# Modulation loads from GpSimd's queue, and seven modulation steps behind each second-gate tile of a two-layer hybrid block

## The chip, the cores and the metric

The kernel runs on one core of one Trainium2 chip. The metric is the device time of one execution in microseconds (us), as the median of three runs. The engines are named as in the profile: PE (TensorE, matmuls), PEld (its weight loads), DVE (VectorE), ACT (ScalarE), POOL (GpSimd) and SP (SyncE, which here only issues DMAs). A q behind an engine's name, as in SPq, is the DMA issue of that engine.

## What is computed

Two layers act on 512 latent tokens and 256 context tokens of width 1024. Each layer derives six modulation vectors per stream from a condition vector, and then computes a gated mixer of three branches and a gated MLP. Cut to what matters here:

```
m = jax.nn.silu(cond) @ ada_w[l] + ada_b[l]          # 6 x 1024, for c and for c_ctx
hx = modulate(rms_norm(x, norm1_g[l]), shift1, scale1)
z  = split_in(hx @ w_in[l])                          # conv, attention, gMLP and 3 x 1024 gate inputs
gates = sigmoid(z_gates + gate_b)
m = gates[0] * y_conv + gates[1] * (attn @ attn_out) + gates[2] * y_sgu
x = x + gate1 * (m @ w_o)
x = x + gate2 * conv_ffn(modulate(rms_norm(x, norm2_g[l]), shift2, scale2))
```

The context stream goes through the first layer whole, and in the second only gives keys and values.

## The kernel before

**Matmuls.** Activations lie with channels on the partitions. Every product is made of three matmuls (lines 468 to 470: high by high, low by high, high by low), so each weight tile is split on chip into a high part, copied by ACT (line 114), and a low part, subtracted by DVE (line 117). Raw weights come in pieces of 1 MB on SP's queue (`load8`, `load4`, `load_ao`, lines 162 to 176) into two buffers named `raw`; the split parts go to a ring named `hl`.

**The stretch that the change touches.** In layer 0 the mixer goes: attention for six tiles of 128 tokens with other matmuls filled in between, then the second gate (`gate(1, j, sg[j])`, eight output tiles j, each with 24 matmuls over 512 latent columns and 24 over 256 context columns), then the product of the attention with `attn_out` (`gated`, eight tiles with half as many matmuls each), then `w_o`. A gate tile ends with an activation by ACT. An `attn_out` tile ends on DVE: line 120 takes it out of PSUM (rows named `g<-g,x` for the 512 latent columns, `g<-g,c` for the 256 context columns), adds it to `m` and splits it for `w_o`. There are two PSUM buffers x and one buffer c here, so the matmuls of the context columns of tile j+1 can start only when DVE has taken tile j out of c.

**The modulation steps.** Only the first vectors of layer 0 are made by matmuls at the start. The others are dot products on DVE, put in behind PE's work: a step loads 128 rows of the transposed weights by 512 columns (256 KB, `t<-in_adat`) into one of four buffers named `t`, and DVE multiplies it with a row of silu that was broadcast over the partitions (`srow<-sd`, also 256 KB, one buffer), and sums it up. Two generators do this. `ada_apart` (lines 342 to 362) makes blocks 16 to 35 of layer 0, first for the context and then for the latent condition, in two halves each: 4 x 20 = 80 steps, with a new `srow` every 20. `ada` (lines 328 to 340) makes blocks 36 to 47 of layer 0 and all blocks of layer 1, later in the program.

**What sets the order.** A call `tick(n)` advances the running generator by n steps; `paced` ties a step to the place of the last matmul written. A scheduler then lays the instructions of every engine out in one fixed order, and each engine and each DMA queue works through its own order without overtaking. In layer 0 the 80 steps of `ada_apart` are ticked 24 times behind the third gate (in the attention), 6 times behind each of the eight second-gate tiles, and once behind each of the eight `attn_out` tiles:

```
        for j in range(8):
            gate(1, j, sg[j])
            tick(6)
        ...
            ms.append((hi, lo))
            tick(1)
        drain()
```

The weight loads of the steps are issued by SP, between the loads of the raw weights; the rows of silu are issued by ACT. GpSimd does nothing but fill 20 small buffers with zeros (line 915, `qT`, for the scores of the attention).

Of the kernel before, what the change touches and what calls it, by code (L numbers as in the profile page):

```python
# [79 lines left out]
def body(tc, I, out):  # L80
    nc = tc.nc
# [8 lines left out]
    def T(p, shape, dt, tag, bufs):  # L90
        return p.tile(shape, dt, tag=tag, name=tag, bufs=bufs)
# [24 lines left out]
    def tt(o, a, b, op):  # L116
        V.tensor_tensor(out=o, in0=a, in1=b, op=op)  # L117
# [13 lines left out]
    def split(hi, lo, src):  # L131
        acopy(hi, src)
        tt(lo, src, f(hi), sub)
# [88 lines left out]
    def page(tag, bufs, dt=F32, n=NT):  # L222
        return T(sp, [128, n], dt, tag, bufs)
# [12 lines left out]
        nc.scalar.dma_start(out=ff, in_=I["ff"][l])  # L236
        return ff

    def bcast_in(t, src):
        nc.scalar.dma_start(out=t, in_=src.unsqueeze(0).broadcast_to([128, src.shape[0]]))  # L240

    def load_rows(l):
        tab = page("t", NTP)
        nc.scalar.dma_start(out=tab[:, :512], in_=I["cst"][:, 512:1024])
        tabC = tab[:, :256].rearrange("p (t d) -> p t d", t=4)
        tabS = tab[:, 256:512].rearrange("p (t d) -> p t d", t=4)
        g = page("t", NTP)
        gq = T(cp, [128, 64], F32, "gq", 1)
        bcast_in(g[:, 0:136], I["qk"][l])
        nsk = T(cp, [128, 8], F32, "nsk", 1)  # L250
        ts(nsk, g[:, 128:136], -1.0, mul)
        ts(gq, g[:, 0:64], 0.125, mul)
        tabs = []
        for i in range(2):
            gg = g[:, 64:128] if i else gq
            tb = T(cp, [128, 512], F32, "tabq", 1) if i == 0 else page("t", NTP)
            tC = tb[:, :256].rearrange("p (t d) -> p t d", t=4)
            tS = tb[:, 256:512].rearrange("p (t d) -> p t d", t=4)
            tt(tC, tabC, gg.unsqueeze(1).broadcast_to([128, 4, 64]), mul)
            for h in range(2):  # L260
                o = lambda t: t.rearrange("p t (a h d) -> p t a h d", a=2, h=2)[:, :, :, h, :]
                gv = gg.rearrange("p (a h d) -> p a h d", a=2, h=2)[:, :, 1 - h, :]
                for t in range(4):
                    tt(o(tS)[:, t], o(tabS)[:, t], gv, mul)
            tabs.append((tC, tS, gg))
        return dict(nsk=nsk, q=tabs[0], k=tabs[1])
# [10 lines left out]
    sd = T(dp, [2, D], F32, "sd", 1)  # L277
# [49 lines left out]
    def ada(l, pool, blocks, both):  # L327

        for h in range(2):
            sr = T(pool, [128, 2, 512], F32, "srow", 1)  # L330
            for c in range(2):
                bcast_in(sr[:, c], sd[c, h * 512:h * 512 + 512])
            for j in blocks:
                w = page("t", NTP)
                nc.sync.dma_start(out=w[:, :512], in_=I["adat"][l, j, :, h * 512:h * 512 + 512])
                yield
                for c in ((1, 0) if j in both else (0,)):
                    o = mods[l][c][:, j:j + 1]
                    paced(V.tensor_tensor_reduce(out=w[:, 512:].bitcast(BF16) if c else w[:, :512], in0=w[:, :512], in1=sr[:, c], scale=1.0,
                                                 scalar=o if h else adab[l][:, j:j + 1], op0=mul, op1=add, accum_out=o))  # L340
                yield

    def ada_apart(l, pool, blocks):


        steps = [(c, h, j) for c in (1, 0) for h in range(2) for j in blocks]

        def load(j, h):
            w = page("t", NTP)
            nc.sync.dma_start(out=w[:, :512], in_=I["adat"][l, j, :, h * 512:h * 512 + 512])  # L350
            return w

        w = load(blocks[0], 0)
        for i, (c, h, j) in enumerate(steps):
            if j == blocks[0]:
                sr = T(pool, [128, 512], F32, "srow", 1)
                bcast_in(sr, sd[c, h * 512:h * 512 + 512])
            yield
            o = mods[l][c][:, j:j + 1]
            paced(V.tensor_tensor_reduce(out=w[:, :512], in0=w[:, :512], in1=sr, scale=1.0,  # L360
                                         scalar=o if h else adab[l][:, j:j + 1], op0=mul, op1=add, accum_out=o))
            if i + 1 < len(steps):
                w = load(steps[i + 1][2], steps[i + 1][1])
# [13 lines left out]
    def tick(n=1):  # L377
        for _ in range(n):
            while bgs:
                try:  # L380
                    g = bgs[0]
                    next(g)
                    if g in bgs:
                        bgs.append(bgs.pop(bgs.index(g)))
                    break
                except StopIteration:
                    bgs.remove(g)

    def drain(g=None):
        while bgs if g is None else g in bgs:  # L390
            tick()
# [4 lines left out]
    def paced(r):  # L396

        if last[0] is not None:
            tc.add_manual_dep(r.ins, last[0].ins.name, SCHED)
# [160 lines left out]
    for l in range(2):  # L560
# [88 lines left out]
        def ab_load(i):  # L649
            if i == 0 and full:  # L650
                ab_load.raw = [raw_tile() for _ in range(2)]
                for h in range(2):
                    for b in range(2):
                        nc.sync.dma_start(
                            out=ab_load.raw[b].rearrange("p (k c) -> p k c", k=8)[:, :, h * 128:h * 128 + 128],
                            in_=I["w_in"][l, :, b * 512 + h * 128:b * 512 + h * 128 + 128].rearrange("(k p) c -> p k c", p=128))
            elif i % 2 == 0:
                ab_load.raw = [load8(I["w_in"][l], b * 512 + i * 128) for b in range(2)]
            PRI[0] = 300
            return [subA(r, i % 2) for r in ab_load.raw]  # L660

        w, t = ab_load(0), page("t", NTP)
# [98 lines left out]
        def gate(b, j, dst):  # L761
            for _ in gate_steps(b, j, dst):
                pass
# [14 lines left out]
        def gated(*a):  # L778
            for _ in gated_steps(*a):
                pass  # L780
# [74 lines left out]
        def Pc_steps():  # L855
            for j in range(8):
                yield from gated_steps(m[j], I["conv_out"][l], j, cv)

        def Gs_steps():
            for j in range(8):  # L860
                t = page("t", NTP) if j >= 2 else early[j]
                if j >= 2:
                    yield from gate_steps(2, j, t)
                tick(2)
                yield from gated_steps(t, I["sgu_out"][l], j, ys)
                tt(m[j][:, :n_m], m[j][:, :n_m], t[:, :n_m], add)
                tick(1)
# [4 lines left out]
        src = [Pc_steps(), Gs_steps()]  # L872
# [138 lines left out]
        if l == 0:  # L1011
            start(ada_apart(0, ap_, range(16, 36)))
# [34 lines left out]
        sg = [sg[j // 2][:, (j % 2) * 768:(j % 2) * 768 + 768] for j in range(8)]  # L1047
        for j in range(8):
            gate(1, j, sg[j])
            tick(6)  # L1050
        Os = list(zip(Oh, Ol))
        ms = []
        for j in range(8):
            gated(sg[j], I["attn_out"][l], j, Os, True)
            tt(m[j][:, :n_m], m[j][:, :n_m], sg[j][:, :n_m], add)
            hi, lo = page("y", 8, F32R), page("m", 8, F32R) if j else page("t", NTP, F32R)
            split(hi[:, :n_m], lo[:, :n_m], m[j][:, :n_m])
            ms.append((hi, lo))
            tick(1)
        drain()  # L1060
        pa.close()

# [32 lines left out]
        if l == 0:  # L1095
            ag = start(ada(0, fp_, range(36, 40), range(48)))
# [22 lines left out]
        if l == 0:  # L1119
            ag = start(ada(0, fp_, range(40, 48), range(48)))  # L1120
# [90 lines left out]
        for ch in range(1, 6):  # L1211
            for j in range(first[ch], first[ch] + sizes[ch]):
                up(j)
                tick(8 if ch == 1 else 12)
            if l == 0 and ch == 1:
                drain(ag)
                start(ada(1, fp_, range(48), range(16)))
            down(down_load(ch - 1), ch - 1, range(8), segs)
# [36 lines left out]
```

## Time and profile before

| | |
|---|---|
| median of three runs | 2097.68 us (2093.98 to 2099.98) |
| the profiled execution, its own time | 2097.33 us |
| its span in the profile | 2095.5 us |
| mean granted TensorE clock | 0.991 of full speed |
| PE busy | 2050.4 us (98% of the span) |
| DVE busy | 1564.9 us (75%) |
| ACT busy | 894.4 us (43%) |
| POOL busy | 10.6 us (1%) |
| HBM read | 215.27 MB, 105 GB/s over the span |

PE is the engine with the most work. The span exceeds its busy time by 45.1 us, and these are the places where a stop of another engine costs time. A busy PE is not PE at its peak, since matmuls are pipelined and a matmul's shown length takes in its wait in the pipe. A row of 25 us in the windows view thus says by how much PE's busy time falls short of 25 where PE stood, and by the granted clock whether it ran at full speed after that.

### The profile page before, as it was taken

The page shows a single profiled execution, that of the slowest core. Times are in us where ns is not written, and L with a number is a line of the kernel's source. Part 1 is how long each engine was busy: PE and PEld are TensorE (multiplying, and loading weights), DVE is VectorE, ACT ScalarE, POOL GpSimd, SP SyncE. Part 2 cuts the span into 40 slices and gives each one's busy share as a digit, 9 for nine tenths or more (in the row PEclk, how much of TensorE's full clock was granted, in tenths as well). Part 3 has the DMA queues.
Part 4 walks back from the last instruction along what each step waited for, and adds up shares of the span by engine and source line. Part 5 has one row for each costly group of instructions (what it writes and reads, how often), then busy time and mean ns, then how long its engine had stood idle before and what let it go on. Part 6 is the DMA issues. An engine that isn't in the chain of part 4 may idle for free.

```text
span 2095.5 us, 29640 instructions
## 1 busy us (share of the span) xinstructions
PE 2050.4 (98%) x11628; PEld 1769.3 (84%) x11628; DVE 1564.9 (75%) x3134; ACT 894.4 (43%) x1485; POOL 10.6 (1%) x24
## 2 busy tenths in 40 slices
PE   6999999999999899999999999999999999999999
PEld 2888898888878898888888898879888888888887
DVE  5689888888667778867595768998987467655654
ACT  5532235677523453323232325433687335333331
POOL 0000000000000000000000000000000000000000
PEclk9999999999999999999999999999999999999999
DMA  8121112213576133444343422322212432222321
GB/s 279 57 81 61 61 61 76 86 55 105 153 220 203 65 101 124 139 141 150 102 141 101 161 78 91 121 65 77 75 46 63 124 126 93 89 92 96 106 99 62
DMA packets 160468, 221.39 MB, mean 106 GB/s; under 512 B 7364, under 2 KB 102340, under 8 KB 160328
## 3 DMA queue, kind: packets, MB, share of 16 engines
q1 hardware_dynamic: 155712, 212.89, 31.5%
q10 hardware_dynamic: 4616, 6.61, 1.0%
q8 instruction: 91, 1.49, 0.3%
q14 instruction: 49, 0.40, 0.1%
HBM read 215.27 MB, written 4.20 MB: 105 GB/s over the span
## 4 chain that ended last, share of the span: by engine, by line
PE 59%; DVE 7%; DMA 4%; ACT 2%; issue 1%; SPq 0%; ACTq 0%; DVEq 0%
PE x L469 8%; PE x L468 8%; PE x L470 8%; PE b L469 7%; PE b L468 7%; PE b L470 7%; DMA t<-in_adat 2%; DVE cy L120 2%; DVE hl L117 2%; PE S L470 2%; PE S L468 2%; PE S L469 2%; PE c L470 2%; PE c L469 2%; PE c L468 2%
## 5 line engine op out<-in xcount | busy, mean ns | idle before, releaser
L114 ACT ACTIVATE hl<-raw 128x1024 fp32r<-128x1024 f32 x264 | 279.2, 1059 | 497.9 <-PE c L469 184.4
L117 DVE TENSOR_TENSOR hl<-raw,hl 128x1024 fp32r<-128x1024 f32 x264 | 322.5, 1222 | 158.8 <-ACT hl L114 156.0
L468 PE MATMUL x<-h,hl 128*128 128x512 f32 (+1 forms) x760 | 292.7, 387 | 6.6 <-ACT h L114 6.6
L470 PE MATMUL x<-h,hl 128*128 128x512 f32 (+1 forms) x760 | 291.7, 385 | 1.4 <-DVE hl L117 1.4
L469 PE MATMUL x<-h,hl 128*128 128x512 f32 (+1 forms) x760 | 292.6, 386 | 0.0
L120 DVE SCALAR_TENSOR_TENSOR cy<-cy,fv 128x503 f32<-128x503 f32 (+29 forms) x240 | 208.5, 880 | 3.0
L469 PE MATMUL b<-h,hl 128*128 128x512 f32 (+1 forms) x552 | 203.9, 370 | 0.0
L468 PE MATMUL b<-h,hl 128*128 128x512 f32 (+1 forms) x552 | 203.5, 370 | 0.0
L470 PE MATMUL b<-h,hl 128*128 128x512 f32 (+1 forms) x552 | 203.2, 369 | 0.3 <-DVE hl L117 0.3
L468 PEld LDWEIGHTS x<-h,hl 128*128 128x128 f32 x760 | 145.3, 192 | 31.0 <-ACT h L114 7.3
L470 PEld LDWEIGHTS x<-h,hl 128*128 128x128 f32 x760 | 145.5, 192 | 27.7 <-DVE hl L117 2.4
L469 PEld LDWEIGHTS x<-h,hl 128*128 128x128 f32 x760 | 145.9, 192 | 23.4 <-DVE h L117 0.3
L470 PEld LDWEIGHTS b<-h,hl 128*128 128x128 f32 x552 | 104.2, 189 | 18.1 <-DVE hl L117 0.7
L468 PEld LDWEIGHTS b<-h,hl 128*128 128x128 f32 x552 | 104.2, 189 | 17.0
L469 PEld LDWEIGHTS b<-h,hl 128*128 128x128 f32 x552 | 104.2, 189 | 16.4
L468 PE MATMUL c<-h,hl 128*128 128x256 f32 x400 | 112.7, 282 | 0.1
L469 PE MATMUL c<-h,hl 128*128 128x256 f32 x400 | 112.5, 281 | 0.1
L470 PE MATMUL c<-h,hl 128*128 128x256 f32 x400 | 112.5, 281 | 0.0
L120 DVE SCALAR_TENSOR_TENSOR m<-b,ff,m 128x511 f32<-128x511 f32 (+2 forms) x118 | 80.8, 688 | 36.1 <-ACT m L1128 34.6
L114 ACT ACTIVATE y<-m 128x512 fp32r<-128x512 f32 (+1 forms) x51 | 36.4, 713 | 128.3 <-DVE m L117 121.8
L468 PE MATMUL b<-y,hl 128*128 128x512 f32 (+1 forms) x256 | 86.3, 338 | 0.7 <-ACT y L114 0.7
L470 PE MATMUL b<-y,hl 128*128 128x512 f32 (+1 forms) x256 | 85.8, 335 | 0.0
(338 smaller groups left out, 4983.0 us busy)
## 6 DMA issues: line engine op xcount, KB each, us to landing
t<-in_adat SPq DMA_DIRECT2D x200, 256.0 KB, 3.4
raw<-in_w_in SPq DMA_DIRECT2D x44, 1024.0 KB, 5.3
raw<-in_ffn_up SPq DMA_DIRECT2D x44, 1024.0 KB, 5.1
raw<-in_ffn_down SPq DMA_DIRECT2D x22, 1024.0 KB, 5.1
raw<-in_w_o SPq DMA_DIRECT2D x8, 1024.0 KB, 7.3
g<-in_xt SPq DMA_DIRECT2D x8, 768.0 KB, 5.5
m<-in_ada SPq DMA_DIRECT2D x16, 256.0 KB, 5.4
h<-in_ada SPq DMA_DIRECT2D x16, 256.0 KB, 5.8
```

Of the source, the lines that this page charges most:

```text
L114: act(out=o, in_=i, func=AF.Copy)
L117: V.tensor_tensor(out=o, in0=a, in1=b, op=op)
L120: return V.scalar_tensor_tensor(out=o, in0=a, scalar=s, in1=b, op0=op0, op1=op1)
L468: nc.tensor.matmul(p, w[0][:, k, cs], hi[:, o:o + n], start=(k == 0), stop=False)
L469: nc.tensor.matmul(p, w[0][:, k, cs], lo[:, o:o + n], start=False, stop=False)
L470: last[0] = nc.tensor.matmul(p, w[1][:, k, cs], hi[:, o:o + n], start=False, stop=(k == nk - 1))
```

## The change

The loads of both generators are issued by GpSimd: those of the modulation weights, which SP issued, and those of the rows of silu, which ACT issued. Seven instead of six steps stand behind each second-gate tile, and none behind an `attn_out` tile: 24 + 56 = 80, as before 24 + 48 + 8 = 80. The other users of `bcast_in` stay on ACT.

```diff
-    def bcast_in(t, src):
-        nc.scalar.dma_start(out=t, in_=src.unsqueeze(0).broadcast_to([128, src.shape[0]]))
+    def bcast_in(t, src, queue=None):
+        (queue or nc.scalar).dma_start(out=t, in_=src.unsqueeze(0).broadcast_to([128, src.shape[0]]))
...
-                bcast_in(sr[:, c], sd[c, h * 512:h * 512 + 512])
+                bcast_in(sr[:, c], sd[c, h * 512:h * 512 + 512], nc.gpsimd)
...
-                nc.sync.dma_start(out=w[:, :512], in_=I["adat"][l, j, :, h * 512:h * 512 + 512])
+                nc.gpsimd.dma_start(out=w[:, :512], in_=I["adat"][l, j, :, h * 512:h * 512 + 512])
...
-            nc.sync.dma_start(out=w[:, :512], in_=I["adat"][l, j, :, h * 512:h * 512 + 512])
+            nc.gpsimd.dma_start(out=w[:, :512], in_=I["adat"][l, j, :, h * 512:h * 512 + 512])
...
-                bcast_in(sr, sd[c, h * 512:h * 512 + 512])
+                bcast_in(sr, sd[c, h * 512:h * 512 + 512], nc.gpsimd)
...
         for j in range(8):
             gate(1, j, sg[j])
-            tick(6)
+            tick(7)
...
             ms.append((hi, lo))
-            tick(1)
         drain()
```

**The order of SP's queue** from the last gate weights to the last `w_o` weights of layer 0, before. `raw` are the weights, `t<-in_adat` the loads of the steps, `g` the residual stream's tiles, and x12 is twelve in a row:

```order
L162 DMA raw<-in_w_in 128x8x256
L350 DMA t<-in_adat 128x512 x12
L176 DMA raw<-in_attn_out 64x4x512 x2
L350 DMA t<-in_adat 128x512 x12
L176 DMA raw<-in_attn_out 64x4x512 x2
L350 DMA t<-in_adat 128x512 x9
L162 DMA raw<-in_w_o 128x8x256
L350 DMA t<-in_adat 128x512 x7
```

In the changed kernel the same place of SP's queue holds the weights alone:

```order
L162 DMA raw<-in_w_in 128x8x256 x5
L176 DMA raw<-in_attn_out 64x4x512 x4
L162 DMA raw<-in_w_o 128x8x256
L530 DMA g_6464<-in_xt 128x1536
L530 DMA g_6465<-in_xt 128x1536
```

All 200 loads of the steps are gone from SP, and no weight load stands between two of them any more.

**The order of POOL's queue** in the attention and the second gate. Before, the zero fills stand alone; they are the - row, and the + rows are the last of the attention and the first of the second gate in the changed kernel:

```order
-L915 MEMSET qT 64x512 x20
+L915 MEMSET qT 64x512
+L350 DMA t<-in_adat 128x512 x3
+L915 MEMSET qT 64x512
+L240 DMA srow<-sd 128x512
+L350 DMA t<-in_adat 128x512 x2
+L915 MEMSET qT 64x512
+L350 DMA t<-in_adat 128x512 x20
+L240 DMA srow<-sd 128x512
+L350 DMA t<-in_adat 128x512 x20
```

The loads of the attention stand between the zero fills, and from the second gate on the queue holds loads alone.

**The order of DVE's work** at the start of `attn_out`, before. `L360` is a step (its second row reads the sum out), `hl` a weight split, and the rows `g_5544<-g_5544,x` and `g_5544<-g_5544,c` take the first `attn_out` tile out of PSUM:

```order
L117 TENSOR_TENSOR hl<-raw,hl 128x1024
L360 ISA t,mod_85<-t,srow,mod_85 128x512
L360 ISA mod_85 128x1
L120 SCALAR_TENSOR_TENSOR g_5544<-g_5544,x 128x512
L360 ISA t,mod_85<-t,srow,mod_85 128x512
L360 ISA mod_85 128x1
L360 ISA t,mod_85<-t,srow,mod_85 128x512
L360 ISA mod_85 128x1
L120 SCALAR_TENSOR_TENSOR g_5544<-g_5544,c 128x256
```

And in the changed kernel:

```order
L117 TENSOR_TENSOR hl<-raw,hl 128x1024
L360 ISA t,mod_85<-t,srow,mod_85 128x512
L360 ISA mod_85 128x1
L120 SCALAR_TENSOR_TENSOR g_5544<-g_5544,x 128x512
L360 ISA t,mod_85<-t,srow,mod_85 128x512
L360 ISA mod_85 128x1
L120 SCALAR_TENSOR_TENSOR g_5544<-g_5544,c 128x256
L360 ISA t,mod_85<-t,srow,mod_85 128x512
L360 ISA mod_85 128x1
```

The rows look alike, but their count ahead differs. Of the 80 steps, 67 stand ahead of the row `g_5544<-g_5544,c` before, and 76 in the changed kernel; 59 and 67 stand ahead of the split of the first `attn_out` weights. Right behind that row three more steps follow, and the 80th stands with the last `attn_out` tile; before, thirteen were spread over `attn_out`.

## Rows read from the trace of the kernel before

**Rows 1.** The page's first part: busy us, share of the span and number of instructions of each engine.
```profile
span 2095.5 us, 29640 instructions
PE 2050.4 (98%) x11628; PEld 1769.3 (84%) x11628; DVE 1564.9 (75%) x3134; ACT 894.4 (43%) x1485; POOL 10.6 (1%) x24
```

**Rows 2.** The windows view in stretches of 25 us, the rows in which PE falls short most (start, middle, end) and one of the MLP. Columns: stretch and its length, busy us of PE, PEld, DVE, ACT and POOL (x instructions), granted clock, mean busy share of the DMA engines, GB/s.
```profile
0.00:25.00 25.00, 14.73 (x42) 3.69 (x42) 8.24 (x18) 12.53 (x20) 0.21 (x4) 1.00 0.93 330
...
600.00:625.00 25.00, 20.31 (x105) 17.57 (x105) 20.09 (x43) 4.33 (x5) 0.00 (x0) 0.86 0.61 191
...
675.00:700.00 25.00, 22.07 (x177) 21.82 (x176) 15.86 (x50) 3.96 (x10) 0.00 (x0) 0.93 0.28 89
700.00:725.00 25.00, 20.99 (x159) 20.09 (x158) 22.89 (x64) 18.69 (x39) 0.00 (x0) 0.93 0.26 85
...
875.00:900.00 25.00, 25.00 (x146) 22.07 (x145) 24.96 (x56) 10.05 (x13) 0.00 (x0) 1.00 0.54 176
```

**Rows 3.** The waits of PE from 590 to 700 us: what waited <- for what, us in total, times, longest.
```profile
PE c L468 <- DVE g L120: 4.7, 1, 4.7
PE x L468 <- DVE g L120: 2.9, 1, 2.9
PE b L468 <- ACT y L114: 0.7, 1, 0.7
```

**Rows 4.** The chain of waits from 560 to 690 us: first its shares by line, then its longest pieces (start us, us, what; a DMA's piece goes from its issue to its landing).
```profile
by line: DMA t<-in_adat 37.2%; DVE t L360 11.8%; issue 10.3%; DVE hl L117 9.3%; DVE m L117 8.8%; DVE g L120 5.8%; DMA srow<-sd 5.8%; DVE t L339 3.9%; PE x L468 1.2%; PE x L469 0.8%; PE x L470 0.8%; ACT hl L114 0.8%; DVE mod L360 0.5%; SPq L
...
571.47 7.01 DMA t<-in_adat
...
588.40 7.95 DMA t<-in_adat
...
649.26 7.27 DMA t<-in_adat
660.26 5.08 DMA t<-in_adat
...
678.80 6.01 DMA t<-in_adat
```

**Rows 5.** DVE from 549.7 to 608.7 us, grouped by line: shapes and count, then busy us and mean ns of one, then the idle time before them and what ended it.
```profile
L360 DVE CUSTOM_DVE_ANT_0 t<-t,srow,adab 128x512 f32<-128x512 f32 x20 | 14.2, 750 | 17.1 <-DMA t<-in_adat 11.8 <-issue 5.3
L360 DVE CUSTOM_DVE_ANT_0 t<-t,srow,mod 128x512 f32<-128x512 f32 x16 | 11.3, 748 | 8.4 <-DMA t<-in_adat 4.3 <-DMA srow<-sd 4.1
```

**Rows 6.** The timeline of DVE in the same stretch: start us, us, instruction, and in brackets the idle time before it and its releaser.
```profile
556.80 0.75 DVE L360 CUSTOM_DVE_ANT_0 t<-t,srow,mod 128x512 f32<-128x512 f32 x1 [3.77 <-DMA t<-in_adat]
...
578.62 0.75 DVE L360 CUSTOM_DVE_ANT_0 t<-t,srow,adab 128x512 f32<-128x512 f32 x1 [4.31 <-DMA t<-in_adat]
...
583.76 0.75 DVE L360 CUSTOM_DVE_ANT_0 t<-t,srow,adab 128x512 f32<-128x512 f32 x1 [0.93 <-DMA t<-in_adat]
...
596.49 0.75 DVE L360 CUSTOM_DVE_ANT_0 t<-t,srow,adab 128x512 f32<-128x512 f32 x1 [5.10 <-DMA t<-in_adat]
...
601.32 0.75 DVE L360 CUSTOM_DVE_ANT_0 t<-t,srow,mod 128x512 f32<-128x512 f32 x1 [4.07 <-DMA srow<-sd]
601.99 0.75 DVE L360 CUSTOM_DVE_ANT_0 t<-t,srow,mod 128x512 f32<-128x512 f32 x1
...
608.41 0.42 DVE L120 SCALAR_TENSOR_TENSOR g<-g,c 128x256 f32<-128x256 f32 x1
```

**Rows 7.** The timeline of PE around the first stop: the first matmul of `attn_out`, the last one before the stop and the first after it.
```profile
596.83 0.40 PE L468 MATMUL x<-cy,hl 128*128 128x512 f32 x1
...
603.80 0.40 PE L470 MATMUL x<-cy,hl 128*128 128x512 f32 x1
...
608.89 0.58 PE L468 MATMUL c<-cy,hl 128*128 128x256 f32 x1 [4.69 <-DVE g L120]
```

**Rows 8.** The windows view behind the two stops, columns as in Rows 2.
```profile
610.00:612.00 2.00, 2.00 (x10) 1.95 (x10) 1.04 (x3) 1.16 (x2) 0.00 (x0) 0.50 1.02 335
612.00:614.00 2.00, 2.00 (x6) 1.57 (x5) 0.00 (x0) 0.74 (x1) 0.00 (x0) 0.50 0.75 285
614.00:616.00 2.00, 2.00 (x11) 1.63 (x11) 1.92 (x6) 0.00 (x0) 0.00 (x0) 0.95 0.12 42
...
686.40:690.00 3.60, 3.60 (x20) 3.60 (x20) 2.33 (x8) 0.83 (x2) 0.00 (x0) 0.60 0.37 123
```

**Rows 9.** The page's list of DMA issues (count, KB each, median us from issue to landing), and the line on landings (min, median, max) of the 36 loads of steps issued from 550 to 609 us.
```profile
t<-in_adat SPq DMA_DIRECT2D x200, 256.0 KB, 3.4
...
srow<-sd ACTq DMA_DIRECT2D x16, 256.0 KB, 4.3
...
DMA to landing us min/median/max: 2.5/4.6/8.1
```

**Rows 10.** The timeline of SP's issues: start us, us, what.
```profile
549.73 0.38 SPq L162 DMA_DIRECT2D raw<-in_w_in  x1
551.05 0.33 SPq L350 DMA_DIRECT2D t<-in_adat  x1
...
570.00 1.37 SPq L176 DMA_DIRECT2D raw<-in_attn_out  x2
571.47 0.55 SPq L350 DMA_DIRECT2D t<-in_adat  x1
```

**Rows 11.** The windows view of three stretches in which DVE waits for such loads, columns as in Rows 2.
```profile
552.00:558.00 6.00, 6.00 (x39) 5.43 (x38) 2.23 (x7) 2.11 (x3) 0.00 (x0) 1.00 0.96 329
574.00:580.00 6.00, 6.00 (x39) 5.42 (x38) 1.69 (x6) 0.69 (x1) 0.00 (x0) 1.00 1.02 272
590.00:596.00 6.00, 6.00 (x37) 5.30 (x36) 1.39 (x3) 0.00 (x0) 0.00 (x0) 1.00 1.06 256
```

**Rows 12.** The waits of POOL over the whole span, the row with the longest wait in the attention proper.
```profile
POOL qT L915 <- PE S L943: 59.7, 3, 34.8
```

## The prediction

> **What bounds the kernel now.** I began with the page's busy times: PE works 98% of the span, and no other engine over 84% [rows 1]. So a change that takes no work off PE can only gain where PE stands. The windows view says where that is: the start, which the change does not touch, a stop at 600 to 625 us, and two at 675 to 725 us [rows 2]. The MLP, where most of the loads that change queue lie, shows PE at 25.00 of 25 us and full clock though DVE is at 24.96 [rows 2]: nothing to gain there.
>
> The waits of PE name the stops from 590 to 700 us: 4.7 us for an instruction of DVE named g, 2.9 us for another, 0.7 us for ACT [rows 3]. Behind the 4.7 us stop the granted clock is 0.50 (1.2 GHz instead of 2.4) until about 614.1 us, behind the 2.9 us stop it is 0.60 on average for 3.6 us [rows 8]. At half speed from 608.9 [rows 7] to 614.1 us PE loses 2.6 us; 0.40 of 3.6 us is 1.4 us. So these places cost 4.7 + 2.6 + 2.9 + 1.4 + 0.7 = 12.3 us, which is all that the change can win if it does nothing else.
>
> What does DVE wait for? The chain of waits from 560 to 690 us hardly touches PE: 37.2% of it are loads `t<-in_adat`, 11.8% the steps that use them [rows 4]. DVE grouped by line shows the same: in the 59 us up to the first stop's end it makes 36 steps and idles 25.5 us before them, 16.1 us for loads, 9.4 us (5.3 of it listed as issue) for the two changes of the silu row [rows 5]. In the timeline the reader is to see that three of the load waits are long, 3.77, 4.31 and 5.10 us, and that the others are at most 0.93 us [rows 6]. Each long one follows a weight load of 1 MB on the same SP queue: the load issued behind `attn_out`'s lands after 7.01 us, another after 7.95 us [rows 4, 10], where the median is 3.4 us [rows 9].
>
> **The change, part by part.**
>
> *Nine more steps ahead of the evacuation that ends the stop (+10.1 us).* PE's 4.7 us stop ends when DVE reaches the row `g<-g,c` at 608.41 us [rows 6, 7]. Ahead of it stand 67 steps now and 76 after the change. A step costs DVE 0.67 us from start to start (601.32 to 601.99) [rows 6], and the average wait for its load is 16.1 / 36 = 0.45 us [rows 5]. Nine times 1.12 is 10.1 us. None of it is hidden: DVE is what PE waits for there. The thirteen steps that leave the rest of `attn_out` were hidden under PE but for the 0.7 us below.
>
> *Loads no longer queue behind weights (-6.6 us).* The three long waits are 13.2 us. On a queue of their own the loads need not wait for a 1 MB weight load to drain, but the bytes stay: the DMA engines are busy 0.96 to 1.06 in these stretches [rows 11]. If two queues share them evenly, the first of four loads lands far earlier and the last about as late as now. I take half, between 0 and 13.2.
>
> *The issue by GpSimd (+6.3 us).* No row shows a DMA from this queue. The nearest row is the load of the same size from another queue than SP's: 4.3 us from ACT against 3.4 us [rows 9]. I charge 0.9 us more from issue to landing. With four buffers the loads come in rounds of four, so DVE pays it once a round: 45 steps are 11 rounds, four of which overlap a weight load and are in the term above; seven times 0.9 is 6.3 us. Ends: 0, and 0.9 on all 11 rounds and both silu rows, 11.7 us. The Trainium skill, page "DMA: Bandwidth & Descriptors", section "Specifications", gives about 1 us to the first byte from GpSimd and 0.6 from SP or ACT; by that 0.4 us this term would be 2.8 and the total 2095.9 us. No run so far shows it.
>
> So DVE reaches that row 10.1 - 6.6 + 6.3 = 9.8 us later than now, and PE's stop grows by that much.
>
> *The slow clock behind the stop (-2.6 us).* The split of the first `attn_out` weights stands behind 67 steps instead of 59, so PE will already stand before `attn_out`, whose first matmul starts at 596.83 us now [rows 7]. Then it does the 7 us of work up to the evacuation at the low clock, in time that it would wait through anyway.
>
> *`w_o` (-5.1 us).* The 2.9 us stop with its 1.4 us of low clock, and the 0.7 us, come from a DVE that is still behind with steps in `attn_out` and then waits for loads queued behind `w_o` and MLP weights (7.27, 5.08 and 6.01 us) [rows 3, 4, 8]. After the change `attn_out` carries four steps instead of thirteen, and the new queue has no weights. I take all of it; the other end is 0. The third stop, at 700 to 725 us, belongs to the norm and stays.
>
> *Priced at nothing.* SP and ACT lose 200 and 16 issues; PE is covered while weights arrive in time, and they do. GpSimd's zero fills now stand between loads; the longest wait of one was 34.8 us [rows 12], and each is needed only for the second half of a tile's scores, so a load ahead of it has time, and the step of a load behind it stands many DVE rows later. In the MLP the loads get the new queue too; the cover is PE's 25.00 of 25 us, and if a load were late there DVE at 24.96 would pass it on.
>
> Sum: +10.1 - 6.6 + 6.3 - 2.6 - 5.1 = +2.1. The profiled execution took 2097.33 us, of which the span is 2095.5; 2097.3 + 2.1 = **2099.4 us**. The median of the runs, 2097.68 us, is 0.35 us above that execution, which changes nothing. A measurement of this kernel can tell about 0.3%, 6.3 us, from no change, so the forecast is: within 0.3%.
>
> **The rivals.**
>
> *The queue was the whole trouble: faster, 2086.5 us.* If loads on their own queue never meet the long waits and GpSimd adds nothing, the terms are 10.1 - 13.2 = -3.1, with -2.6 and -5.1: -10.8. For it: every long wait follows a weight load. Against it: the engines are full in just those stretches [rows 11]. Chance 0.24.
>
> *GpSimd's issue is slow: slower, 2107.1 us.* The wait behind PE's stop is not removed but takes another form: each load leaves later, DVE waits once a round, and the split and the evacuation behind it on DVE come later. At 2 us more for seven rounds the term is 14 instead of 6.3, the total +9.8. It decides from 10.5 us, 1.5 us per round, on (then the total is 6.3). For it: a DMA issue has never run on this engine here. Against it: another queue costs 0.9. Chance 0.17.
>
> *The bytes are the limit: slower, 2106.0 us.* If a second queue brings no load earlier, the -6.6 goes: +8.7. For it: busy shares of 0.96 to 1.06 [rows 11], and nine steps more in the same stretch are 2.3 MB more. Against it: 329 GB/s is reached in one of these stretches and 256 in another, so there is room. The same page of the Trainium skill, section "Issuing engines are not separate DMA queues", says that DMAs of all issuing engines run on the same 16 engines and interleave, so that a second issuer saves only issue time; by that rule this is the case. The issue times here are 0.33 us or little more [rows 10], so there is little of that to save. Chance 0.12.
>
> *GpSimd's queue tangles in the attention: slower, about 2114 us.* Nine times there a load stands behind a zero fill that waits for PE. If each came a landing (3.4 us) too late, DVE would lose some 30 us; at half of that passed on to PE it is 15 more, less what DVE catches up. The order speaks against it. Chance 0.05.
>
> *The change does not empty `attn_out`.* That is so in part, and counted: four of the steps still stand behind the first evacuation.
>
> **How the numbers follow.** The forecast has what the rivals leave, 0.42. Faster by over 0.3%: 0.24. Slower by over 0.3%: 0.17 + 0.12 + 0.05 = 0.34. Low end 2087, about the first rival. High end: +10.1, no gain from the queue, and 11.7 for GpSimd with nothing saved after it is +21.8, 2119; all that at once is unlikely, so I stop at 2115, which takes in the last rival. Range 2087 to 2115 us.
>
> **What would show it.** In the profile after: the loads of steps land at 4 to 4.5 us, and those that meet weights at 5 to 6, not 7 to 8. From 550 us DVE makes 44 or 45 steps up to `g<-g,c`, which it reaches near 618 us, not 608. PE stands some 10 to 15 us in all between 580 and 620 us, in two or more pieces, and not at 683 us; POOL's zero fills wait no longer than now. I am wrong if DVE reaches that row before 612 us (then the queue was the trouble), if it does so after 623 us or the MLP shows PE below 25.00 (then GpSimd's issue is slow), or if the stop near 683 us is still there.

## The result and the profile after

The changed kernel takes 2108.41 us (median of six runs, 2107.03 to 2110.61), the kernel before 2097.97 us (six runs beside it). It is slower by 10.4 us or 0.5% by the medians; the ratio estimated from all the runs is 1.006, with a 95% interval of 1.0048 to 1.0072. The measured time lies within the range of 2087 to 2115 us, but the forecast of 2099.4 us, within 0.3% of before, did not come true. The profiled execution took 2107.83 us, 10.5 us more than that of before.

PE has the same 11628 matmuls, and stands longer. The page's first part, after, answers to [rows 1]:

```profile
span 2106.1 us, 29670 instructions
PE 2055.3 (98%) x11628; PEld 1772.6 (84%) x11628; DVE 1567.2 (74%) x3134; ACT 893.9 (42%) x1485; POOL 127.1 (6%) x240
```

Busy times hide the loss. POOL is up by 116 us, the time of its 216 new issues. The windows view, columns as in [rows 2], shows the place:

```profile
550.00:575.00 25.00, 24.24 (x141) 21.19 (x140) 12.79 (x33) 6.33 (x9) 9.11 (x17) 1.00 0.62 204
575.00:600.00 25.00, 20.41 (x100) 17.25 (x99) 12.60 (x33) 4.22 (x6) 8.30 (x16) 0.86 0.81 219
600.00:625.00 25.00, 17.25 (x90) 14.17 (x88) 14.12 (x35) 2.11 (x3) 8.37 (x16) 0.93 0.80 245
625.00:650.00 25.00, 22.19 (x119) 19.53 (x120) 22.07 (x30) 8.95 (x10) 0.54 (x1) 0.93 0.45 154
675.00:700.00 25.00, 24.30 (x184) 22.91 (x183) 17.56 (x47) 5.78 (x10) 3.76 (x7) 1.00 0.49 160
...
875.00:900.00 25.00, 25.00 (x147) 22.04 (x146) 24.33 (x54) 9.31 (x12) 4.83 (x9) 1.00 0.51 180
```

PE falls short by 15.9 us between 550 and 650 us. The stop at 675 to 700 us has shrunk from 2.9 us [rows 2] to 0.7, and the MLP stands at 25.00 as before: with the loads on another queue nothing changed there. The timeline of PE has four stops of over 2 us in that stretch (start us, us, instruction, idle time before it and its releaser):

```profile
584.84 0.80 PE L470 MATMUL x<-h,hl 128*128 128x512 f32 x1 [4.59 <-DVE hl L117]
...
608.40 0.80 PE L470 MATMUL x<-cy,hl 128*128 128x512 f32 x1 [3.75 <-DVE hl L117]
619.24 0.39 PE L468 MATMUL c<-cy,hl 128*128 128x256 f32 x1 [2.71 <-DVE g L120]
627.81 0.39 PE L468 MATMUL c<-cy,hl 128*128 128x256 f32 x1 [4.10 <-DVE g L120]
```

All four end with DVE: two weight splits that stand behind too many steps, then the rows that take the first and the second `attn_out` tile out of PSUM. Behind the first, second and fourth the granted clock is at the lower of its two levels, 1.2 instead of 2.4 GHz, for 3 to 6 us, while around the third it stays full (windows view):

```profile
584.90:593.00 8.10, 8.10 (x24) 6.44 (x25) 5.79 (x15) 0.00 (x0) 3.49 (x7) 0.63 0.70 238
608.40:612.00 3.60, 3.60 (x10) 2.93 (x11) 2.81 (x7) 0.00 (x0) 1.38 (x3) 0.58 0.72 237
615.00:620.00 5.00, 2.29 (x13) 1.69 (x12) 4.84 (x11) 0.00 (x0) 2.18 (x5) 1.00 0.77 234
628.00:632.00 4.00, 4.00 (x17) 3.61 (x17) 4.00 (x6) 1.50 (x2) 0.00 (x0) 0.57 0.23 73
```

A ledger follows from setting each matmul against the one with the same number in the kernel before. This is how much later it starts, from the two timelines:

| place in PE's order, start now | later than before by |
|---|---|
| second gate, 571.6 us | -0.7 us |
| behind the first stop, 584.8 | +4.2 |
| behind its low clock, 591.0 | +7.2 |
| behind the second stop, 608.4 | +11.1 |
| the first `c<-cy` behind the third stop, 619.24 (608.89 before, [rows 7]) | +10.35 |
| where before had its low clock [rows 8], 622.2 | +7.99 |
| behind the fourth stop, 627.8 | +12.2 |
| behind its low clock, 656.8 | +13.9 |
| where before had the stop near 683 us and its low clock, 697.8 | +8.9 |
| last matmul | +10.45 |

The ledger starts below zero because in this execution PE was already 1.5 us ahead of before at 75 us, in the start that the change does not touch. From a common start the change adds up to 12.0 us in this pair of executions.

DVE reaches the row `g<-g,c` of the first tile at 618.77 us, 608.41 before [rows 6], and then three more steps follow. The third of them waits 4.31 us:

```profile
618.77 0.41 DVE L120 SCALAR_TENSOR_TENSOR g<-g,c 128x256 f32<-128x256 f32 x1
...
620.12 0.75 DVE L360 CUSTOM_DVE_ANT_0 t<-t,srow,mod 128x512 f32<-128x512 f32 x1 [0.27 <-DMA t<-in_adat]
...
625.20 0.75 DVE L360 CUSTOM_DVE_ANT_0 t<-t,srow,mod 128x512 f32<-128x512 f32 x1 [4.31 <-DMA t<-in_adat]
```

That wait is PE's fourth stop. The load was issued a microsecond behind 1 MB of `w_o`, and landed after 7.08 us (timelines of SP's and GpSimd's issues):

```profile
616.93 0.38 SPq L162 DMA_DIRECT2D raw<-in_w_o  x1
617.98 0.54 POOL L350 DMA_DIRECT2D t<-in_adat  x1 [1.27 <-DVE mod L360]
```

So the loads did not escape the weights. The page's line on DMA issues and the line on landings (min, median, max) of the four loads issued from 572 to 576 us, behind two issues of `attn_out` weights at 571.60 us:

```profile
t<-in_adat POOLq DMA_DIRECT2D x200, 256.0 KB, 3.4
```
```profile
DMA to landing us min/median/max: 7.0/8.1/8.1
```

The median from GpSimd is 3.4 us as from SP [rows 9], and behind weights a load takes as long as it did on the weights' own queue (up to 8.1 us, [rows 9]).

### The profile page after: what moved, and what is told of

Its sections match the earlier page's. It is cut to its first block, busy times and chain, and to the rows that moved or that the text cites. A ratio compares the mean times of both kernels' runs of the same rounds, so it can differ in the third digit from the quotient of the medians.

```text
span 2106.1 us, 29670 instructions
## 1 busy us (share of the span) xinstructions
PE 2055.3 (98%) x11628; PEld 1772.6 (84%) x11628; DVE 1567.2 (74%) x3134; ACT 893.9 (42%) x1485; POOL 127.1 (6%) x240
## 4 chain that ended last, share of the span: by engine, by line
PE 76%; DVE 10%; issue 6%; DMA 3%; ACT 3%; POOL 1%; ACTq 0%; POOLq 0%; SPq 0%; DVEq 0%
PE x L469 9%; PE x L470 9%; PE x L468 9%; PE b L469 8%; PE b L468 8%; PE b L470 8%; DVE cy L120 3%; PE c L469 2%; PE c L468 2%; PE c L470 2%; DVE hl L117 2%; PE b L980 2%; PE S L468 2%; PE S L469 2%; PE S L470 2%
## 5 line engine op out<-in xcount | busy, mean ns | idle before, releaser
L335 POOL DMA_DIRECT2D t<-in_adat x120 | 64.5, 537 | 506.0 <-DVE mod L339 250.4
L468 PE MATMUL b<-y,hl 128*128 128x512 f32 (+1 forms) x256 | 86.2, 337 | 0.0
```

Of the source, the lines that this page charges most:

```text
L335: nc.gpsimd.dma_start(out=w[:, :512], in_=I["adat"][l, j, :, h * 512:h * 512 + 512])
L468: nc.tensor.matmul(p, w[0][:, k, cs], hi[:, o:o + n], start=(k == 0), stop=False)
```

## The experiments

Times of before stand beside each group: 2096.27 us for the first four, 2096.51 for the next three, 2097.14 for the last two. For the stretch in question a table is put together from the timelines of DVE: from the first weight split of the second gate (31 or 32 steps stand ahead of it) to the first row `g<-g,c`. The last column is needed because the profiled executions differ before any edit acts: it says how far PE was ahead of before at 75 us, in the start that all these kernels share. It shifts the time at which the row is reached, but not the length of the stretch.

| kernel | its steps | us | of it waits of steps | row reached at | time of the kernel | PE ahead at 75 us |
|---|---|---|---|---|---|---|
| before | 36 | 59.9 | 25.6 | 608.41 | 2097.97 | 0 |
| after | 44 | 71.7 | 31.1 | 618.77 | 2108.41 | 1.5 |
| old places, GpSimd (1) | 38 | 67.9 | 31.4 | 613.97 | 2104.13 | 2.6 |
| new places, SP and ACT (2) | 39 | 62.7 | 23.6 | 607.73 | 2098.29 | 3.5 |
| order by hand, GpSimd (5) | 35 | 63.0 | 28.7 | 608.43 | 2100.64 | 3.2 |
| before, but `ada` from GpSimd (8) | 36 | 60.6 | 25.8 | 606.85 | 2099.53 | 2.2 |
| order by hand, only `ada_apart` from GpSimd (9) | 35 | 62.9 | 28.7 | 611.38 | 2102.29 | 0.2 |

**1. The queue alone.** The changed kernel with the old counts:

```diff
-            tick(7)
+            tick(6)
...
             ms.append((hi, lo))
+            tick(1)
```

> The loads are issued by GpSimd as in the changed kernel, the steps are placed as before (six behind each second-gate tile, one behind each attn_out tile). In DVE's order 69 steps stand ahead of the row g<-g,c that takes the first attn_out tile, 67 before, 76 in the changed kernel. Theory (the bytes are the limit, the queue is neutral, each step ahead costs 1.1 us): DVE reaches that row near 611 us, loads issued just before a weight load still land after 6 to 8 us, time 2096 to 2102 us. Rival one (GpSimd's issue is what costs): most of the 10.4 us remains, 2105 to 2109 us. Rival two (the queue helps and only the seventh step hurts): 2088 to 2094 us.

2104.13 us, ratio 1.0031 (1.0018 to 1.0044). This lies between theory and rival one, and nearer to the rival: moving the queue, with what that does to DVE's order, costs 7.9 us by the medians, 6.5 by the ratio. Rival two is out. The execution profiled was the fastest of the twelve (2098.58 us), so its trace is used for lengths and places and not for the total. In it the stretch is 8.0 us longer than before, with two steps more.

**2. The places of the steps alone.** The kernel before with the new counts:

```diff
-            tick(6)
+            tick(7)
...
             ms.append((hi, lo))
-            tick(1)
```

> The steps are placed as in the changed kernel (seven and none), the loads stay on SP and the rows of silu on ACT. 71 steps stand ahead of the row g<-g,c of the first attn_out tile, five more follow before the third tile. Theory (steps cost, the queue is neutral): that row is reached near 613 us, another stop of 3 to 5 us follows behind the second or third tile, time 2102 to 2107 us. Rival one (GpSimd's issue is what costs): 2095 to 2100 us. Rival two (the queue helps): slower than the changed kernel, 2110 us or more.

2098.29 us, ratio 1.0004 (0.9991 to 1.0017): no difference. Theory falls (the row came at 607.73 us, not near 613, and no second stop followed), rival one holds its number. The new places are not free on the way, though: the stretch is 2.8 us longer than before, PE's stop at the row 7.7 us instead of 4.7, and the stop near 683 us 1.9 us instead of 2.9, which gives a part back.

But the order is not that of the changed kernel. Here 71 steps stand ahead of the row, there 76, and 60 instead of 67 ahead of the first `attn_out` split. The scheduler is the same and only the queue differs; a likely reason, which no run shows, is that it places a step by when it reckons its load to land, and reckons that loads on SP queue behind the weights. The counts ahead of the row are 67 before, 69 with the queue alone (1), 71 with the places alone and 76 with both, so two and four steps come from each part, and three only from the two together. The times do not tell as clearly whether the two parts simply add up: the queue alone costs 6.5 us, the places alone 0.8 and both 12.6 by the ratios, and 7.9, 2.0 and 10.4 by the medians. Of the fourth stop, 4.1 us in the changed kernel, kernel 1 has 1.8 us and kernel 2 nothing.

**3. The last four steps out of the way.** The changed kernel with

```diff
-            tick(7)
+            tick(7 if j < 7 else 3)
...
             ms.append((hi, lo))
+            if j >= 4:
+                tick(1)
```

> The changed kernel with its last four steps moved: three instead of seven steps behind the last second-gate tile, and one behind each of the last four attn_out tiles. 75 steps stand ahead of the first row g<-g,c, and the next comes only behind the fourth tile. Theory: PE's 4.1 us stop at 622 us and the low clock behind it come from one step whose load met the first w_o weights, so both go, 5.9 us less: 2102 to 2104 us, with the first row still reached near 618 us. Rival: DVE is late there anyway, and the stop only moves to a later attn_out tile or into w_o: 2107 to 2110 us.

2103.3 us, ratio 1.0029 (1.0017 to 1.0042), 5.1 us less than the changed kernel by the medians, 6.5 by the ratios, where 5.9 less was expected. The waits of PE from 540 to 760 us (us in total, times, longest):

```profile
PE x L470 <- DVE hl L117: 9.1, 3, 4.6
PE c L468 <- DVE g L120: 2.1, 1, 2.1
```

After has 9.1 in three and 6.8 in two. The splits' stops are untouched, the first row is reached at 618.74 us, and of the two waits for `g` the one of 4.1 us is gone: the matmul that is 13.9 us later than before in after is 7.9 later here. The theory holds.

**4. A quarter of the bytes.** The changed kernel, its `ada_apart` with

```diff
-            nc.gpsimd.dma_start(out=w[:, :512], in_=I["adat"][l, j, :, h * 512:h * 512 + 512])
+            nc.gpsimd.dma_start(out=w[:, :128], in_=I["adat"][l, j, :, h * 512:h * 512 + 128])
...
-            paced(V.tensor_tensor_reduce(out=w[:, :512], in0=w[:, :512], in1=sr, ...
+            paced(V.tensor_tensor_reduce(out=v4(w[:, 512:].bitcast(BF16)), in0=w[:, :128].unsqueeze(1).broadcast_to([128, 4, 128]), in1=v4(sr), ...
```

(`v4` views 512 columns as four times 128.)

> The changed kernel with a quarter of the bytes in the loads of ada_apart: 128 of 512 columns are loaded and read four times by a step of the same size, so three quarters of those weights are left out. Same number of loads, same issues, same order. Theory (the bytes of loads and weights together are the limit): loads land after 2 to 2.5 us, those issued with a weight load after less than 4.5 us; DVE's waits for loads and silu rows between 550 us and the first g<-g,c fall from 35 to under 20 us, that row is reached before 605 us, and the time is 2086 to 2094 us. Rival (what costs is the fixed time from issue to landing, or the place behind the weights' descriptors): landings stay above 3 and above 6 us with weights, the time stays above 2103 us.

2092.04 us, ratio 0.9971 (0.996 to 0.9983), 16 us less than the changed kernel and within theory's 2086 to 2094; the row is reached at 611.40 us, not before 605, and DVE's waits in the stretch from 549.7 us are 21.1 us, where under 20 were expected. PE's waits for splits and for `g` from 540 to 760 us are 4.2 us, 15.9 in after. The page's line on the issues, and the landings of the four loads issued behind the `attn_out` weights (571 to 575 us; the weights at 570.90 and 571.66):

```profile
t<-in_adat POOLq DMA_DIRECT2D x80, 64.0 KB, 2.2
```
```profile
DMA to landing us min/median/max: 5.9/6.5/6.9
```

The median load takes 2.2 us instead of 3.3, so bytes count, as the theory said. Behind weights it still takes 6.5 us with a quarter of the bytes. If the queues shared the engines evenly, 64 KB would be through long before 1 MB. The DMA view from 572 to 576 us shows what happens instead. Of the queues (kind: packets, MB, share of the 16 engines) it lists one, SP's, though four loads have been issued by GpSimd:

```profile
q1 hardware_dynamic: 362, 0.71, 89.6%
t<-in_adat POOLq DMA_DIRECT2D x4, 64.0 KB, 6.5
```

So in these 4 us no packet of a load started, while 0.71 MB of the weights moved. It is the weights' bytes that a load waits for, on whichever of the two queues it stands; there the rival is right, and the step of the prediction that took half of 13.2 us falls.

**5. The order of before, on GpSimd.** The changed kernel with counts chosen so that the splits of the second gate stand behind 31, 37, 43, 47, 55, 59 and 64 steps, as before:

```diff
-            tick(7)
+            tick((6, 6, 6, 4, 8, 4, 5, 4)[j])
...
             ms.append((hi, lo))
+            tick((2, 2, 2, 0, 2, 1, 1, 3)[j])
```

> All loads from GpSimd, and the steps placed by hand so that DVE's order from the first second-gate tile to the first attn_out tile is that of the kernel before (31, 37, 43, 47, 55, 59 and 64 steps ahead of the weight splits, 66 instead of 67 ahead of the first row g<-g,c). Theory one (GpSimd's queue costs nothing by itself; what cost was the order of DVE that the scheduler makes for it, with more steps ahead of the splits and of that row): the row is reached between 606 and 610 us, the stop near 683 us is gone, 2091 to 2097 us. Theory two (a queue of its own costs by itself, since loads no longer wait for the weights' place in line and land later, or leave later): the row is reached between 612 and 616 us as with all loads on GpSimd and the old places, 2100 to 2106 us.

2100.64 us, ratio 1.0019 (1.0009 to 1.003), 3.5 us less by the medians, 2.5 by the ratios, than with the order that the scheduler made in (1). The timeline of DVE:

```profile
607.15 0.68 DVE L120 SCALAR_TENSOR_TENSOR g<-g,x 128x512 f32<-128x512 f32 x1
608.43 0.42 DVE L120 SCALAR_TENSOR_TENSOR g<-g,c 128x256 f32<-128x256 f32 x1
```

The row is reached as theory one said, but the time is theory two's. The table tells why: PE was 3.2 us ahead at 75 us, so the stretch began 3.1 us earlier here, and it took 3.1 us longer, with one step less. So with this order held, GpSimd's queue costs some 3 us of waiting in it. Kernel 9, with the same order and without the early start, shows the same: 62.9 us, and the row at 611.38. The stop near 683 us did not go (2.4 us).

Behind the row the order is not that of before, and a stop of 2.6 us in `w_o` is new (DVE's and PE's timelines):

```profile
647.28 0.75 DVE L360 CUSTOM_DVE_ANT_0 t<-t,srow,mod 128x512 f32<-128x512 f32 x1 [2.26 <-DMA t<-in_adat]
648.49 0.39 PE L468 MATMUL S<-y,hl 128*128 128x256 f32 x1 [2.60 <-DVE g L120]
```

It is the 80th step. Its load left at 642.13 us, a microsecond behind 768 KB of `g<-in_xt` on SP, and landed after 5.12 us; the row of `g` that PE needs stands right behind the step on DVE. Before, that step starts at 644.25 us without a wait, two splits ahead of this row. So part of what this kernel loses comes from the place of one step, as with the fourth stop of the changed kernel.

**6, 7. Sixteen steps more in the attention.** The kernel before with

```diff
-                tick(2)
+                tick(3)
...
-                tick(1)
+                tick(2)
...
-            tick(6)
+            tick(4)
...
-            tick(1)
+            tick((0, 0, 0, 1, 1, 1, 1, 1)[j])
```

and, in 6, the weight loads of `ada` issued by GpSimd, in 7 by SP as before. Of the 80 steps, 40 now stand in the attention, 32 behind second-gate tiles, 5 behind `attn_out` tiles and 3 behind them all.

> The loads of ada_apart on SP as before, those of ada on GpSimd; 40 steps in the attention instead of 24 (three and two a tile instead of two and one), four behind each second-gate tile, none behind the first three attn_out tiles, one behind each later one. 71 steps stand ahead of the first row g<-g,c, but about 29 instead of 36 of them behind the last split of the attention. Theory (steps left for the second gate times 1.65 us set when that row is reached): it is reached near 597 us, before PE wants it, so the stop at 604 us and its low clock go; the stop at 683 us goes with ada's loads on their own queue; 2085 to 2091 us. Rival (DVE has no room for sixteen more steps in the attention, and PE loses there what it wins): PE's busy time falls by 5 us or more between 400 and 550 us, 2095 us or more.

> The same places of the steps, with all loads on SP. Theory: only the stop near 683 us tells it from the kernel with ada's loads on GpSimd, 3 to 4 us: 2089 to 2094 us. Rival: that stop comes from DVE being late with its steps in attn_out, not from loads behind w_o on SP, and is gone here too: the two are equal within 1 us.

6: 2093.74 us, ratio 0.9983 (0.9974 to 0.9991), not within the 2085 to 2091 expected. 7: 2090.37 us, ratio **0.996** (0.9945 to 0.9974), within the 2089 to 2094 expected, and faster than both kernels of this case. The row is reached at 600.91 and 600.74 us (597 expected). The attention took the sixteen steps: from 400 to 550 us PE is busy 149.0 us in 6 and 149.1 in 7, 149.2 before, so the rival to 6 falls. What 7 wins and where it gives part of it back (windows, then the longest wait of PE from 540 to 760 us):

```profile
600.00:625.00 25.00, 25.00 (x146) 21.96 (x146) 21.82 (x36) 7.64 (x9) 0.00 (x0) 1.00 0.61 198
675.00:700.00 25.00, 19.65 (x153) 19.40 (x152) 15.11 (x47) 8.50 (x19) 0.00 (x0) 0.93 0.18 56
```
```profile
PE x L468 <- DVE g L120: 5.3, 1, 5.3
```

The stop at 604 us is gone. The one near 683 us grew from 2.9 to 5.3: PE comes to it some 8 us earlier, and DVE is not ready. On that stop theory and rival of both were wrong: it went neither with `ada`'s loads on GpSimd (3.6 us in 6) nor with them on SP (5.3 in 7). By the medians 6 is 3.4 us slower than 7, but their profiled executions end within 0.8 us of each other, so the traces do not show where that lies.

**8. `ada`'s loads alone on GpSimd**, all else as before:

```diff
-                nc.sync.dma_start(out=w[:, :512], in_=I["adat"][l, j, :, h * 512:h * 512 + 512])
+                nc.gpsimd.dma_start(out=w[:, :512], in_=I["adat"][l, j, :, h * 512:h * 512 + 512])
                 yield
```

> The kernel before, with the 120 weight loads of ada alone moved to GpSimd; the loads of ada_apart, all rows of silu and the places of the steps stay. Theory one (a queue without weights spares ada's loads the wait behind w_o on SP): PE's stop of 2.9 us near 683 us and the low clock behind it go, 2091 to 2095 us. Theory two (what GpSimd's queue costs beside the order in the second gate, some 4 us, lies with ada's loads, in w_o or after): 2099 to 2102 us. Neither: 2095 to 2098 us.

2099.53 us, ratio 1.0011 (1.0 to 1.0022), within theory two's range. The stop, in PE's timeline, is not gone but longer, and DVE's timeline names a load issued behind MLP weights (5.95 us to landing) as its longest wait for a load:

```profile
687.45 0.58 PE L468 MATMUL x<-y,hl 128*128 128x256 f32 x1 [4.74 <-DVE g L120]
```
```profile
668.02 0.75 DVE L339 CUSTOM_DVE_ANT_0 t<-t,srow,adab 128x512 bf16<-128x512 f32 x1 [5.38 <-DMA t<-in_adat]
```

Theory one falls: the queue does not cure this stop, which is 4.7 instead of 2.9 us.

**9. `ada_apart` alone on GpSimd**: kernel 5 with the loads and rows of `ada` back on SP and ACT, by the line of 8 the other way round.

> The kernel whose steps were placed by hand for GpSimd's queue, with ada's loads and its rows of silu back on SP and ACT, so that GpSimd issues the 80 loads of ada_apart and its rows alone. Theory one (the rest of some 4 us lies with ada's loads): 2095 to 2098 us. Theory two (it lies with the loads of ada_apart and the way the steps stand in attn_out): 2099 to 2102 us.

2102.29 us, ratio 1.0027 (1.0014 to 1.004): just above theory two's range, and no less than kernel 5. So what is left there does not lie with `ada`'s loads, though by 8 these cost 2.3 us by the ratio (0 to 4.6) when they move alone. In `w_o` the 80th step waits here as in 5 (2.54 us), and PE 2.9 us for the row behind it.

## Why the prediction was right or wrong

| term | predicted | measured |
|---|---|---|
| (already there at 75 us, before any edit acts) | | -1.5 |
| nine more steps ahead of the row | +10.1 | } |
| no wait behind weights | -6.6 | } +11.9 together (618.77 - 608.41, and the 1.5) |
| issue by GpSimd | +6.3 | } |
| low clock behind the stop | -2.6 | -2.4 (+10.35 to +7.99) |
| `w_o` | -5.1 | -5.0 (+13.9 to +8.9) |
| four steps behind the row | 0 | +5.9 (+7.99 to +13.9) |
| rest, up to the last matmul | 0 | +1.6 |

The range held the time, but the forecast was no difference, and the kernel is slower. **The step that failed** is the sentence that `attn_out` is emptied "in part, and counted" (in the rival on `attn_out`): its four remaining steps were counted in number and given no price. One of their loads left just behind the first `w_o` weights, DVE waited 4.31 us for it with the second tile's row queued behind, PE stood 4.1 us and then ran at the low clock. Experiment 3 took that wait away and got back 5.1 us by the medians, 6.5 by the ratios, of the 5.9. With it the sum would have been +8.0, slower by over 0.3%.

**The first three terms** give +9.8 where +11.9 came, close only because two errors cancel in part. "Half of 13.2 us" for loads on a queue of their own was wrong: kernel 4 shows a load of a quarter of the bytes still waiting 6.5 us behind weights. That is the mechanism of the third rival, "the bytes are the limit" (2106.0 us). The Trainium skill's page "DMA: Bandwidth & Descriptors", section "Issuing engines are not separate DMA queues", says the same of a second issuer, that only issue time is saved; the trace agrees on the waits (7.0 to 8.1 us behind `attn_out` weights on either queue), but issue time was not saved: 0.54 us an issue on GpSimd, 0.33 on SP. The term for GpSimd's issue, +6.3, was too high. The landings (min, median, max) of the 80 loads of `ada_apart`, from SP before and from GpSimd after:

```profile
DMA to landing us min/median/max: 2.5/3.3/8.1
```
```profile
DMA to landing us min/median/max: 2.7/3.3/8.1
```

They differ by 0.2 us at the least and not in the middle. With the order held the stretch is 3.1 us longer (5 against before). After against 2, which has five steps less, it is 9.0 us longer, and five steps at 1.37 us (0.67 and a wait of 25.6 / 36) are 6.9, which leaves 2; in 1 against before, two steps more, 5 us are left. So GpSimd costs an estimated 2 to 5 us in the stretch, with no one wait to blame: several of 0.3 to 1.7 us. One source of this cost stands ahead of the issue, where the term did not look. When its queue stands free, a load's issue starts 0.41 us after the end of the step that frees its buffer on GpSimd, 0.04 us on SP (medians in the stretch; 0.41 in all of after, 1, 3, 4, 5 and 9, 0.04 in before, 2 and 8). Paid once for each four loads, 0.37 us is 3.3 us over 36 steps, an estimate of the size of the 3.1.

**Nine steps at 1.12 us** was the right count, and near the right price. The prediction did not say where they came from. The new places alone give four of them (71 against 67) and the queue alone two; the other three come only with both, since the scheduler puts more steps ahead of the splits when the loads are on GpSimd. The four by themselves cost no time that can be measured (2): what they cost at the row, the stop near 683 us gives back in part.

**`w_o`** has its size for a wrong reason. The prediction put it down to loads queued behind weights on SP. But on GpSimd the stop stays where PE is early (8: 4.74 us, with PE 2.0 us early ahead of `w_o`) and shrinks to about 0.5 us or less where PE is late (after: 13.9 us late; 1: 7.7 us; 3: 7.9 us). It is slack. PE goes on there at 686.4 us before, 684.4 in 2, 687.5 in 8, wherever PE stood ahead of it: what DVE has to do up to that row sets the time. So, up to the length of the stop, what PE loses at 580 to 630 us it does not lose again at 683, and what kernel 7 wins it partly gives back (680.9 us).

**Of the signs named ahead**, these came: PE's 11.05 us of stops between 580 and 620 us in three pieces (10 to 15 forecast), the row near 618 us, no stop near 683 us (0.2 us), the zero fills' longest wait (still 34.8 us among the scores), MLP at 25.00. These did not: landings of 4 to 4.5 us (3.3 in the middle), and of 5 to 6 behind weights (5.7 to 8.1). None of the signs of being wrong came, although the kernel is slower: the list had none for the rows behind the first.

**Open**: how the scheduler comes to its order; how GpSimd's 2 to 5 us divide between the later issue and another meeting with the weights, since neither was tried by itself; and what makes kernel 6 slower than 7.

## What to carry to other kernels

Moving loads to another engine's queue can change three things: where they wait, how soon they leave, and where a scheduler puts the work that uses them. Compare the orders with only the one part changed before pricing the whole. A load that started just behind a large one was late on either queue here, so look for a place or a time without large ones: sixteen steps moved into the attention brought 6 us by the medians, 8 by the ratio. And work that is left behind a critical row is not free because it is little: price the load it waits for, and the rows that are queued behind it.

## What was not expected of the hardware

A load of 64 KB on GpSimd's queue, issued 0.3 to 2.5 us behind the second of two of 512 KB on SP's, landed after 5.9 to 6.9 us, where the median is 2.2 us. From 572 to 576 us no packet of GpSimd's queue started. So in these runs a large transfer that had been issued first was not overtaken from another queue, neither by loads of 64 KB nor by those of 256 KB.

Where the queue stood free, an issue on GpSimd started 0.41 us after the step that freed its buffer, on SP 0.04 us, in every kernel named above.
